# Low parts of the U and V tiles in the dense stage: from GpSimd to the vector engine

## The chip, the cores and the metric

One core of one Trainium2 chip runs the whole program. Its engines are TensorE (PE, matmuls), the vector engine (DVE), ScalarE (ACT), GpSimd (POOL) and SyncE (SP, which here only issues DMAs). The metric is the device time of one execution, in microseconds. Three runs of the kernel before took 3260.62, 3271.71 and 3278.69 us (median 3271.71).

## The reference

The reference is one layer of a hybrid backbone: two gated mixers, an output projection, and then a feed-forward block called PEER. Only the last part matters here:

```
def retrieve(xb):                                   # 128 tokens at a time, 1024 in all
    q = (xb @ wq).reshape(128, 8, 2, 128)
    s = einsum('tphq,phkq->tphk', q, keys)          # 2 x 128 keys per head
    top_s, top_i = top_k(s, 16)
    ...                                             # 16 best pairs per head: idx, softmax g
    act = gelu(einsum('tpkd,td->tpk', u_tab[idx], xb))
    return einsum('tpk,tpkd->td', g * act, v_tab[idx])
```

Each token has 8 heads with 16 experts each, 128 in all, out of a table of 16384 experts. An expert is a row of U (1024 numbers) and a row of V (1024 numbers). The result goes through a gate, a residual addition and a final RMSNorm.

## The kernel before

The eight blocks of 128 tokens are split. Three blocks (the gather blocks, A) fetch the rows of their experts from memory. Five blocks (the dense blocks, B, 640 tokens) multiply with the whole U and V tables on TensorE, with a weight of zero for every expert that a token did not choose.

*The gather* is a generator (`gather_all`) of 3 x 128 steps, one per block and expert position. A step fetches, for each of the 128 tokens, one row of U and V (128 x 2048 numbers) by an indirect DMA that GpSimd issues (L936), two steps ahead, into one of four buffers `uv`. The vector engine multiplies the U half with the hidden state and sums (L983); ScalarE makes the activation from the sum (L948, L949); one step later the vector engine adds activation times V half to the accumulator `acc` (L961). The fetch into a buffer waits for the addition L961 that read it last. The gather's steps are spread over the other work by a count of time (`ticks`).

*The dense side* goes through the experts in 128 chunks of 128. `u_side(c)` multiplies one U chunk with the hidden state of the five blocks (48 matmuls, L1017); ScalarE's gelu of that is `w` (L1058). 84 of the chunks are done before the dense stage and wait in memory; the other 44 are done in it. `weights(c)` multiplies `w` with the routing weights (vector engine, L1376). The V product adds `w` times the V chunk to the output (L1403).

*High and low parts.* Each matmul operand of full precision is split in two: ScalarE rounds the tile to the matmul's type (`uh`, `vh`, `wh`), and a subtraction gives the rest, the low part (`ul`, `vl`, `wl`). A product is three matmuls: high x high, high x low, low x high. In the kernel before, GpSimd makes `ul` (L1043) and `vl` (L1369, and L1362 for the last five tiles), the vector engine makes `wl` (L1380).

*The dense stage* begins at about 1889 us. It goes through 16 groups of eight chunks; each group has two halves (the two halves of V's 1024 columns). In a half-group TensorE does eight steps of 5 x 3 matmuls into five PSUM banks of six; at its end the vector engine adds the five banks to the output accumulator (L1410). The second half also makes the next group's weights and, for some chunks, their U product. In step n the kernel issues, behind the matmuls of the first token block, the rounding and the low part of the V tile for step n + 2 (`v_prep`, three buffers each for `vh` and `vl`), and SP loads the raw tile for step n + 7 (five buffers). In the last group there is no next group, and the vector engine and GpSimd finish the residual.

The order of the instructions on each engine is the order in which the program issues them: nothing is rearranged.

Of the kernel before, what the change touches and what calls it, by code (L numbers as in the profile page):

```python
# [7 lines left out]
F32 = mybir.dt.float32  # L8
# [6 lines left out]
ALU = mybir.AluOpType  # L15
# [845 lines left out]
def peer(tc, A, F, order, ng, out, ahi, alo, eh, ga, h2s, h2_load, early=84, rho=0.42, rhog=0.33, ratio=1.35, lead=6.0, sige=0.2):  # L861
# [5 lines left out]
    V, S, T, G, Y = nc.vector, nc.scalar, nc.tensor, nc.gpsimd, nc.sync  # L867
    banks, ident, dr, rstd_of = [F["bank"]], F["ident"], F["dr"], F["rstd_of"]
    bank = lambda name: banks[0](name)
# [51 lines left out]
    def settle(n):  # L921

        t = row("acc")
        for h in range(2):
            S.activation(t[:, h * 512:h * 512 + 512], accs[n][:, h * 512:h * 512 + 512], AF.Copy)
        accs[n] = t
# [92 lines left out]
            if kt % 2:  # L1019
                yield 2 * 3 * sum(b - a for a, b in cuts) / 2400.0  # L1020

    us, wr, ubank, ulim = {}, {}, [bank], [early + 1]

    first = [c for c in range(P) if (c + 1) * early // P != c * early // P]
    plan = first + [c for c in range(P) if c not in first]
# [9 lines left out]
    def u_prep(c):  # L1035
        if c >= P or isinstance(us[c], tuple):
            return
        uh = up.tile([P, KT, P], F32R, tag="uh", name="uh")
        ul = up.tile([P, KT, P], F32R, tag="ul", name="ul")
        for n, ur in enumerate(us[c]):  # L1040
            k = slice(4 * n, 4 * n + 4)
            S.activation(uh[:, k], ur, AF.Copy)  # L1042
            G.tensor_tensor(ul[:, k], ur, uh[:, k].bitcast(F32), op=ALU.subtract)  # L1043
        us[c] = (uh, ul)

    def u_side(c, ahead):

        cuts = cuts_of(nd)
        pts = [ubank[0]("ua") for _ in cuts]
        for n, d in enumerate(project(pts, None, us[c][0], us[c][1], bhi, blo, cuts)):  # L1050
            if ahead and n == 0:
                u_prep(c + 1)
            if ahead and n == 1:
                u_load(c + (3 if c + 1 < early else 2))
            yield d
        w = wr[plan[c]] = up.tile([P, nd], F32, tag="we", name="w", bufs=3)
        for pt, (a, b) in zip(pts, cuts):
            S.activation(w[:, a:b], pt[:, :b - a], AF.Gelu)  # L1058
# [133 lines left out]
    def prime():  # L1192

        u_load(0)
        u_load(1)
        u_load(2)
        u_prep(0)
# [116 lines left out]
    acc = hB2.tile([P, nb, D], F32, name="accB")  # L1314
    ru[0] = es.enter_context(tc.tile_pool(name="ru2", bufs=2))
    ulim[0] = P
    for n in list(accs):
        if accs[n] is psum[0]:
            settle(n)
# [6 lines left out]
    with tc.tile_pool(name="vhl", bufs=3) as vp, tc.tile_pool(name="whl", bufs=GRP) as wp, \  # L1326
            tc.tile_pool(name="gw", bufs=2) as gw:
        ws, vs, gts, vr = {}, {}, {}, {}
# [23 lines left out]
        def v_last(n):  # L1352

            if not halves:
                for _ in range(2):
                    th, tl = (up.tile([P, KT, P], F32R, tag=t, name="v" + t).rearrange("p (a k) e -> p a (k e)", a=2)
                              for t in ("uh", "ul"))
                    halves.extend((th[:, a], tl[:, a]) for a in range(2))
                halves.append([up.tile([P, nd], F32R, tag="we", name="vw", bufs=3)[:, :512] for _ in range(2)])
            vh, vl = vs[n] = halves.pop(0)  # L1360
            S.activation(vh, vr[n], AF.Copy)
            G.tensor_tensor(vl, vr.pop(n), vh.bitcast(F32), op=ALU.subtract)  # L1362

        def v_prep(n):
            if n < len(vseq) - NX:
                vh = vp.tile([P, 512], F32R, tag="vh", name="vh")
                vl = vp.tile([P, 512], F32R, tag="vl", name="vl")
                S.activation(vh, vr[n], AF.Copy)  # L1368
                G.tensor_tensor(vl, vr.pop(n), vh.bitcast(F32), op=ALU.subtract)  # L1369
                vs[n] = (vh, vl)  # L1370

        def weights(c):
# [39 lines left out]
        def v_ahead(n):  # L1412
            v_prep(n + 2)
            if n + 7 < len(vseq) - NX:
                v_load(n + 7)
# [40 lines left out]
        for c in groups[0]:  # L1456
            produce(c)
            if c == 2:
                for n in range(2):
                    v_prep(n)  # L1460
                    v_load(n + 5)
        n = 0
        for g, group in enumerate(groups):
            nxt = groups[g + 1] if g + 1 < len(groups) else []
            for h in range(2):
# [3 lines left out]
                for i, c in enumerate(group):  # L1469
                    for b in range(nb):  # L1470
                        v_mm(pos[b], n, c, b, i == 0, i == len(group) - 1)
                        if nxt and i == len(group) - 1 and b >= HOLD:
                            owed[0] += t1 * share_of * (1.0 if h else ratio)
                        elif nxt:
                            ticks(t1, share_of * (1.0 if h else ratio))
                        else:
                            k = i * nb + b
                            if k < cut:
                                rest(cut - k)
                            j = k - cut  # L1480
                            if j >= 0 and j % 3 == 0 and j // 3 < nb:
                                x1_load(j // 3)
                            j -= 8
                            if j >= 0 and j % 3 == 0 and j // 3 < nb:
                                residual(j // 3, 1)
                        if b == 0:
                            v_ahead(n)
                        if b == 1:
                            weigh()
                        if b == 3 and not nxt:  # L1490
                            if 1 <= i < 1 + NX:
                                v_last(len(vseq) - NX - 1 + i)
                            if i < NX:
                                v_load(len(vseq) - NX + i)
                    n += 1
                    if h and i < len(nxt):
                        produce(nxt[i])
                for b in range(nb):
                    v_add(g, h, b, pos[b])

        v_prep(n + 2)

        def second(b, po):
# [28 lines left out]
def whole(tc, A, out, ng=8, dbg=None):  # L1532
# [32 lines left out]
    e2.close()  # L1565
    es.close()
    peer(tc, A, r, order, ng, out, ahi, alo, eh, ga, h2s, h2_load)
    r["es"].close()

# [55 lines left out]
```

## Time and profile before

| | |
|---|---|
| runs, us | 3260.62, 3271.71, 3278.69 |
| profiled execution, us | 3258.37 |
| its span, us | 3256.6 |
| mean granted TensorE clock | 0.945 |
| busy share: PE, DVE, ACT, POOL | 89%, 79%, 40%, 49% |
| dense stage | about 1889 us to the end |

Busy shares are averages over stages that are limited by different things. The stage around the change is read from its own stretch, by who waits for whom. An engine's instruction can overlap the end of the one before it by some 0.08 us, so that the time from start to start is a little less than the duration.

### The profile page before, as it was taken

To read this page: it belongs to the slowest core of one execution; us is meant where nothing else is said; L and a number is where in the kernel's file an instruction comes from. 1 tells how busy PE (TensorE), PEld (TensorE's weight loads), DVE (VectorE), ACT (ScalarE), POOL (GpSimd) and SP (SyncE) were. 2 spreads that over 40 slices of the span, in tenths; PEclk is the share of its full clock that TensorE was granted. 3 is DMA by queue.
4 is the path that set the end of the run, shared out by engine and by line. 5 is a ranking of instruction groups with operands and counts; after the bars stand their busy time and mean duration, and the time that the engine had idled before them with its cause. 6 is when DMAs were issued, how large, how long until landed. Compare 5 with 4: busy or idle time off the path is not lost.

```text
span 3256.6 us, 47765 instructions
## 1 busy us (share of the span) xinstructions
PE 2895.9 (89%) x17321; PEld 2560.1 (79%) x17321; DVE 2583.2 (79%) x4467; ACT 1304.8 (40%) x2909; POOL 1581.0 (49%) x1102
## 2 busy tenths in 40 slices
PE   6999989998988987798888889989998899999897
PEld 3899887777988987688887877777777777778775
DVE  6633418666898999999999778888888788888886
ACT  4622224453444455455555433333333233333232
POOL 1000002333456766644343466666665566667664
PEclk9999999799998998899999999999999899999999
DMA  5254437345377876689898999999988898999883
GB/s 204 71 182 143 142 110 261 123 134 178 120 261 267 286 261 238 218 283 322 314 320 310 353 318 318 315 319 310 311 301 308 302 321 305 321 315 320 305 294 126
DMA packets 374381, 831.44 MB, mean 255 GB/s; under 512 B 27001, under 2 KB 198649, under 8 KB 324737
## 3 DMA queue, kind: packets, MB, share of 16 engines
q0 software_dynamic: 57600, 411.07, 35.0%
q1 hardware_dynamic: 292624, 347.74, 33.6%
q10 hardware_dynamic: 23920, 69.59, 5.5%
q8 instruction: 136, 2.23, 0.3%
q14 instruction: 101, 0.82, 0.1%
HBM read 729.38 MB, written 98.91 MB: 254 GB/s over the span
## 4 chain that ended last, share of the span: by engine, by line
DVE 21%; issue 11%; PE 10%; POOL 9%; DMA 5%; ACT 1%; SPq 0%; POOLq 0%; DVEq 0%; ACTq 0%
PE po L1403 7%; POOL vl L1369 4%; DVE ol L1296 4%; POOL uv L936 4%; DVE uv L983 4%; PE ua L1017 3%; DVE acc L961 3%; DMA uv<-uv,idx 3%; DVE accP L961 2%; DVE oh L1297 2%; DVE oh L1295 2%; DVE o L1294 2%; DVE w L1376 1%; DMA vr<-uv 1%; ACT wh L1379 1%
## 5 line engine op out<-in xcount | busy, mean ns | idle before, releaser
L936 POOL DMA_INDIRECT uv<-uv,idx x384 | 512.9, 1336 | 548.2 <-DVE accP L961 237.3
L983 DVE SCALAR_TENSOR_TENSOR uv<-uv,h2a 128x1024 f32<-128x1024 f32 x351 | 543.9, 1550 | 106.7 <-DMA uv<-uv,idx 106.5
L1403 PE MATMUL po<-vh,wh 128*128 128x512 f32 x1255 | 509.5, 406 | 118.4 <-DVE accB L1410 106.0
L1403 PE MATMUL po<-vl,wh 128*128 128x512 f32 x1255 | 507.1, 404 | 16.4 <-POOL vl L1369 16.4
L1017 PE MATMUL ua<-hBhi,uh 128*128 128x320 f32 x2048 | 487.2, 320 | 36.9 <-ACT uh L1042 30.3
L1403 PE MATMUL po<-vh,wl 128*128 128x512 f32 x1255 | 503.8, 401 | 0.0
L1017 PE MATMUL ua<-hBhi,ul 128*128 128x320 f32 x2048 | 478.4, 315 | 21.2 <-POOL ul L1043 20.9
L1369 POOL TENSOR_TENSOR vl<-vr,vh 128x512 fp32r<-128x512 f32 x251 | 387.2, 1545 | 198.4 <-ACT vh L1368 177.9
L1017 PE MATMUL ua<-hBlo,uh 128*128 128x320 f32 x2048 | 477.1, 315 | 0.0
L1043 POOL TENSOR_TENSOR ul<-ur,uh 128x512 fp32r<-128x512 f32 x256 | 391.9, 1553 | 171.3 <-ACT uh L1042 164.4
L961 DVE SCALAR_TENSOR_TENSOR acc<-uv,act,acc 128x1024 f32<-128x1024 f32 x237 | 398.3, 1681 | 8.5 <-ACT act L949 8.5
L1403 PEld LDWEIGHTS po<-vh,wh 128*128 128x128 f32 x1255 | 246.2, 196 | 179.8 <-DVE accB L1410 115.4
L1017 PEld LDWEIGHTS ua<-hBhi,uh 128*128 128x128 f32 x2048 | 352.0, 194 | 44.3 <-ACT uh L1042 32.9
L1017 PEld LDWEIGHTS ua<-hBhi,ul 128*128 128x128 f32 x2048 | 351.3, 193 | 26.9 <-POOL ul L1043 26.9
L1017 PEld LDWEIGHTS ua<-hBlo,uh 128*128 128x128 f32 x2048 | 352.6, 193 | 0.0
L1403 PEld LDWEIGHTS po<-vl,wh 128*128 128x128 f32 x1255 | 246.3, 196 | 72.0 <-POOL vl L1369 22.3
L1403 PEld LDWEIGHTS po<-vh,wl 128*128 128x128 f32 x1255 | 245.5, 196 | 53.0
L1379 ACT ACTIVATE wh<-w 128x640 fp32r<-128x640 f32 x128 | 94.6, 739 | 465.5 <-DVE w L1376 465.5
L1368 ACT ACTIVATE vh<-vr 128x512 fp32r<-128x512 f32 x251 | 156.5, 625 | 186.7 <-PE po L1403 156.1
L948 ACT ACTIVATE act<-act 128x1 f32<-128x1 f32 x384 | 76.1, 198 | 353.8 <-DVE uv L983 352.1
L468 POOL MEMSET v<- 128x4 f32 x20 | 2.0, 105 | 419.1 <-PE tm L207 383.7
L1380 DVE TENSOR_TENSOR wl<-w,wh 128x640 fp32r<-128x640 f32 x128 | 113.3, 885 | 104.8 <-ACT wh L1379 100.8
(375 smaller groups left out, 5920.5 us busy)
## 6 DMA issues: line engine op xcount, KB each, us to landing
ur<-uC SPq DMA_DIRECT2D x256, 256.0 KB
vr<-uv SPq DMA_DIRECT2D x256, 256.0 KB
d_G<-gtl ACTq DMA_DIRECT2D x80, 512.0 KB
gch<-d_G SPq DMA_DIRECT2D x64, 640.0 KB
d_A<-w ACTq DMA_DIRECT2D x84, 320.0 KB
w<-d_A SPq DMA_DIRECT2D x84, 320.0 KB
wm<-w_mod SPq DMA_DIRECT2D x32, 512.0 KB
qraw<-wq SPq DMA_DIRECT2D x32, 512.0 KB
```

Source lines behind the costliest of these rows:

```text
L936: G.indirect_dma_start(out=t.rearrange("p a d -> p (a d)"), out_offset=None, in_=A["uv"], in_offset=bass.IndirectOffsetOnAxis(ap=idxs[n][: ...
L948: S.activation(acts[i], acts[i], AF.Gelu)
L961: V.scalar_tensor_tensor(acc, v, act, acc, op0=ALU.mult, op1=ALU.add)
L983: V.scalar_tensor_tensor(t, t, 1.0, h2s[n], op0=ALU.mult, op1=ALU.mult, accum_out=acts[i])
L1017: T.matmul(pt[:, :b - a], l[:, kt], m[:, kt, a:b], start=(kt == 0 and wi == 0), stop=(kt == KT - 1 and wi == 2))
L1043: G.tensor_tensor(ul[:, k], ur, uh[:, k].bitcast(F32), op=ALU.subtract)
L1296: V.tensor_tensor(ol, oh, pairs(glT, b, t0), op=ALU.mult)
L1368: S.activation(vh, vr[n], AF.Copy)
L1369: G.tensor_tensor(vl, vr.pop(n), vh.bitcast(F32), op=ALU.subtract)
L1379: S.activation(wh, w, AF.Copy)
L1380: V.tensor_tensor(wl, w, wh.bitcast(F32), op=ALU.subtract)
L1403: T.matmul(po, st[:, b * P:(b + 1) * P], m, start=(start and wi == 0), stop=(stop and wi == 2))
```

## The change

In the dense stage the subtractions that make `ul` and `vl` move from GpSimd to the vector engine. Before the dense stage `ul` stays on GpSimd. Nothing else is altered; the subtractions stand at the same places of the program.

```
-    us, wr, ubank, ulim = {}, {}, [bank], [early + 1]
+    us, wr, ubank, ulim, usplit = {}, {}, [bank], [early + 1], [G]
...
             S.activation(uh[:, k], ur, AF.Copy)
-            G.tensor_tensor(ul[:, k], ur, uh[:, k].bitcast(F32), op=ALU.subtract)
+            usplit[0].tensor_tensor(ul[:, k], ur, uh[:, k].bitcast(F32), op=ALU.subtract)
...
     ulim[0] = P
+
+    usplit[0] = V
...
             S.activation(vh, vr[n], AF.Copy)
-            G.tensor_tensor(vl, vr.pop(n), vh.bitcast(F32), op=ALU.subtract)
+            V.tensor_tensor(vl, vr.pop(n), vh.bitcast(F32), op=ALU.subtract)
...
                 S.activation(vh, vr[n], AF.Copy)
-                G.tensor_tensor(vl, vr.pop(n), vh.bitcast(F32), op=ALU.subtract)
+                V.tensor_tensor(vl, vr.pop(n), vh.bitcast(F32), op=ALU.subtract)
```

The vector engine's queue in the first half of a group, from the five additions on, in the kernel before (`uv`, `act`, `acc` are the gather, `w` and `wl` a weight):

```order
L1410 TENSOR_TENSOR accB<-accB,po 128x512 x5
L983 SCALAR_TENSOR_TENSOR uv,act<-uv,h2a 128x1024
L961 SCALAR_TENSOR_TENSOR acc<-uv,act,acc 128x1024
L1376 TENSOR_TENSOR w<-w,gch 128x640
L1380 TENSOR_TENSOR wl<-w,wh 128x640
L983 SCALAR_TENSOR_TENSOR uv,act<-uv,h2a 128x1024
L961 SCALAR_TENSOR_TENSOR acc<-uv,act,acc 128x1024
L983 SCALAR_TENSOR_TENSOR uv,act<-uv,h2a 128x1024
L961 SCALAR_TENSOR_TENSOR acc<-uv,act,acc 128x1024
```

The same place now (line numbers behind the change are two higher, so L1412 is the former L1410, L1371 the former L1369):

```order
L1412 TENSOR_TENSOR accB<-accB,po 128x512 x5
L983 SCALAR_TENSOR_TENSOR uv,act<-uv,h2a 128x1024
L961 SCALAR_TENSOR_TENSOR acc<-uv,act,acc 128x1024
L1371 TENSOR_TENSOR vl<-vr,vh 128x512
L1378 TENSOR_TENSOR w<-w,gch 128x640
L1382 TENSOR_TENSOR wl<-w,wh 128x640
L983 SCALAR_TENSOR_TENSOR uv,act<-uv,h2a 128x1024
L961 SCALAR_TENSOR_TENSOR acc<-uv,act,acc 128x1024
L1371 TENSOR_TENSOR vl<-vr,vh 128x512
L983 SCALAR_TENSOR_TENSOR uv,act<-uv,h2a 128x1024
L961 SCALAR_TENSOR_TENSOR acc<-uv,act,acc 128x1024
L1371 TENSOR_TENSOR vl<-vr,vh 128x512 x2
```

One subtraction of a V tile stands in each of the eight steps between the gather's instructions. GpSimd's queue at about the same place, before (`uv` is a fetch):

```order
L936 DMA uv<-uv,idx_7051 128x2048
L1369 TENSOR_TENSOR vl<-vr,vh 128x512
L936 DMA uv<-uv,idx_7051 128x2048
L1369 TENSOR_TENSOR vl<-vr,vh 128x512
L1043 TENSOR_TENSOR ul<-ur,uh 128x512 x2
L936 DMA uv<-uv,idx_7051 128x2048 x2
L1369 TENSOR_TENSOR vl<-vr,vh 128x512 x2
```

And now, from the last U tile before the dense stage to the residual at the end:

```order
L1043 TENSOR_TENSOR ul<-ur,uh 128x512 x2
L936 DMA uv<-uv,idx_7051 128x2048 x108
L936 DMA uv<-uv,idx_7052 128x2048 x128
L1445 TENSOR_TENSOR accB<-accB,ft 128x512
L1446 TENSOR_TENSOR accB<-accB,fx 128x512
```

All fetches of the dense stage now stand directly behind one another.

## Rows read from the trace of the kernel before

**Rows 1.** Busy us (and instructions) of PE, PEld, DVE, ACT, POOL by stretch; PEclk, DMA share, GB/s

```profile
1840.00:1880.00 40.00, 37.42 (x253) 36.76 (x252) 18.07 (x20) 12.96 (x35) 22.34 (x17) 1.00 1.01 380
1896.00:3216.00 1320.00, 1186.48 (x5692) 1015.10 (x5690) 1110.39 (x1117) 420.91 (x1033) 867.62 (x567) 0.95 0.89 307
```

**Rows 2.** Waits of PE, 1896 to 3216: us in total, times, longest us

```profile
PE po L1403 <- DVE accB L1410: 106.0, 21, 7.8
```

**Rows 3.** Waits of DVE, same stretch

```profile
DVE wl L1380 <- ACT wh L1379: 97.6, 119, 2.0
DVE uv L983 <- DMA uv<-uv,idx: 86.0, 53, 4.1
```

**Rows 4.** DVE by line, same stretch: busy us, mean ns | idle before, releaser

```profile
L961 DVE SCALAR_TENSOR_TENSOR acc<-uv,act,acc 128x1024 f32<-128x1024 f32 x234 | 394.4, 1685 | 1.7 <-ACT act L949 1.7
L983 DVE SCALAR_TENSOR_TENSOR uv<-uv,h2a 128x1024 f32<-128x1024 f32 x234 | 387.5, 1656 | 86.1 <-DMA uv<-uv,idx 86.0
L1376 DVE TENSOR_TENSOR w<-w,gch 128x640 f32<-128x640 f32 x124 | 152.3, 1228 | 6.7 <-ACT w L1058 6.7
L1380 DVE TENSOR_TENSOR wl<-w,wh 128x640 fp32r<-128x640 f32 x124 | 109.8, 886 | 101.6 <-ACT wh L1379 97.6 <-issue 4.0
L1410 DVE TENSOR_TENSOR accB<-accB,po 128x512 f32<-128x512 f32 x140 | 85.9, 677 | 0.0
```

**Rows 5.** Chain that ended last, a piece: start us, us, what

```profile
2197.07 6.83 PE po L1403 x30
2203.90 7.04 PE ua L1017 x48
```

**Rows 6.** DVE in order of time, one half-group: start us, us, instruction, [idle before]

```profile
2239.73 3.07 DVE L1410 TENSOR_TENSOR accB<-accB,po 128x512 f32<-128x512 f32 x5
2242.72 1.22 DVE L983 SCALAR_TENSOR_TENSOR uv<-uv,h2a 128x1024 f32<-128x1024 f32 x1
...
2243.86 1.28 DVE L961 SCALAR_TENSOR_TENSOR acc<-uv,act,acc 128x1024 f32<-128x1024 f32 x1
2245.06 0.82 DVE L1376 TENSOR_TENSOR w<-w,gch 128x640 f32<-128x640 f32 x1
...
2247.43 1.22 DVE L983 SCALAR_TENSOR_TENSOR uv<-uv,h2a 128x1024 f32<-128x1024 f32 x1
...
2251.94 1.27 DVE L961 SCALAR_TENSOR_TENSOR acc<-uv,act,acc 128x1024 f32<-128x1024 f32 x1
2253.14 2.31 DVE L983 SCALAR_TENSOR_TENSOR uv<-uv,h2a 128x1024 f32<-128x1024 f32 x1
...
2265.31 1.58 DVE L983 SCALAR_TENSOR_TENSOR uv<-uv,h2a 128x1024 f32<-128x1024 f32 x1 [4.10 <-DMA uv<-uv,idx]
...
2272.86 0.67 DVE L1410 TENSOR_TENSOR accB<-accB,po 128x512 f32<-128x512 f32 x1
```

**Rows 7.** Gather lines, 1896 to 3216: ns min/median/max, first and last start, forms

```profile
L983 DVE SCALAR_TENSOR_TENSOR uv<-uv,h2a x234: 1208/1225/3228, 1898.3 to 3172.6; 128x1024 f32<-128x1024 f32 x117
L961 DVE SCALAR_TENSOR_TENSOR acc<-uv,act,acc x234: 1271/1282/2382, 1900.5 to 3178.3; 128x1024 f32<-128x1024 f32 x117
```

**Rows 8.** POOL in order of time, same half-group

```profile
2251.14 1.69 POOL L936 DMA_INDIRECT uv<-uv,idx  x1 [1.35 <-DVE acc L961]
2252.85 3.75 POOL L1369 TENSOR_TENSOR vl<-vr,vh 128x512 fp32r<-128x512 f32 x2
2256.74 1.76 POOL L936 DMA_INDIRECT uv<-uv,idx  x1
```

**Rows 9.** POOL by line, 1896 to 3216

```profile
L1369 POOL TENSOR_TENSOR vl<-vr,vh 128x512 fp32r<-128x512 f32 x248 | 382.2, 1543 | 198.4 <-ACT vh L1368 177.9 <-ACT act L948 14.8 <-DMA fx<-d_x 2.0
L1043 POOL TENSOR_TENSOR ul<-ur,uh 128x512 fp32r<-128x512 f32 x82 | 147.1, 1814 | 78.7 <-ACT uh L1042 78.6
```

**Rows 10.** Multiplication of two SBUF tiles in the tail, whole run

```profile
L1443 DVE TENSOR_TENSOR accB<-accB,ft x5: 679/1757/1772, 3198.1 to 3216.9; 128x512 f32<-128x512 f32 x5
```

**Rows 11.** Waits of ACT, 1896 to 3216

```profile
ACT vh L1368 <- PE po L1403: 156.1, 85, 2.9
```

## The prediction

> **What bounds the kernel now.** The views were read in this order: the page's busy shares, the busy time of each engine in stretches, the waits by engine, the groups by line for the vector engine and GpSimd, and the timeline of one half-group. The change acts from about 1889 us on, so only the dense stage counts. In its 1320 us from 1896 to 3216 TensorE is busy 1186 us, the vector engine 1110 us and GpSimd 868 us, and the DMA engines are at 0.89 of their time [rows 1]. No engine is full, so the reader has to look at who waits for whom.
>
> TensorE's longest wait is 106 us, for the additions that empty its PSUM banks (L1410, vector engine) [rows 2]. The vector engine waits 97.6 us for ScalarE's rounding of a weight (L1380) and 86.0 us for gathered rows [rows 3]. What it does not wait for says most: its 140 additions L1410 have 0.0 us of idle time before them [rows 4]. Whenever it comes to them, TensorE has long finished. The vector engine, with its busy time and its short waits, is therefore the late engine at nearly every half-group's end, and TensorE stands until it arrives. A half-group is eight weight chunks times five token blocks. Each chunk gives a block three matmuls, so a half is 120 of them; 30 take 6.83 us, so it needs 27.3 us, and a U chunk 7.04 us more [rows 5]. The half from 2239.73 to 2272.86 has no U chunk and took 33.1 us [rows 6].
>
> Much of the vector engine's busy time is not work. Its two gather instructions have medians of 1225 and 1282 ns [rows 7] but means of 1656 and 1685 ns [rows 4]. The timeline shows why. A product that starts at 2253.14 takes 2.31 us; GpSimd has just begun a pair of low parts, at 2252.85, which runs 3.75 us. An addition at 2251.94 takes 1.27 us although GpSimd issues a fetch from 2251.14 on, for 1.69 us [rows 6, 8]. So GpSimd's subtractions hold the vector engine up, and its fetches do not.
>
> **The change part by part.** *Leaves GpSimd:* 248 V and 82 U low parts in this stretch [rows 9] (five more of the last V tiles lie in the tail). *Arrives on the vector engine:* the same 330 subtractions, 128x512, each behind ScalarE's rounding. The trace has no such subtraction of two SBUF tiles there. The nearest row is the multiplication of two SBUF tiles of that size, 679 ns at best [rows 10]; L1410 of that size takes 677 ns alone [rows 4], and five in a row take 3.07 us [rows 6], so one more in a row costs (3.07 - 0.677) / 4 = 0.60 us, as ends overlap the next start. The two ends are 330 x 0.60 = 198 us and 330 x 0.679 = 224 us. I take 198, since the queue runs without gaps most of the time.
>
> *What goes with them:* the blocking. By the unblocked prices (the medians; 0.82 us for a 128x640 multiplication, from 2245.06 [rows 6], taken for L1380 too) and the means of [rows 4] that is 234 x (1.656 - 1.225) = 101, 234 x (1.685 - 1.282) = 94, 124 x (1.228 - 0.82) = 51 and 124 x (0.886 - 0.82) = 8, in all 254 us. Net on the vector engine: 198 - 254 = -56 us, with -30 as the other end.
>
> The page Perfetto Trace Analysis of the Trainium skill, section Optimizing Scalar/DVE Operations, advises the reverse: when the vector engine is saturated, hand work to ScalarE or even GpSimd; it adds that the two share an SBUF read port, so that it might not help. Taken alone, the first half would make this change a loss of the whole 198 us; the 2.31 us beside 1.27 us in the trace speaks for the second half. The sum above uses neither.
>
> *Fetches:* GpSimd's queue now holds fetches alone until the tail. Before, a fetch stands behind subtractions: that of 2256.74 behind the pair of 2252.85 [rows 8]. The product at 2265.31 then waits 4.10 us for its rows [rows 6]; the buffer that the fetch needed had been free since the addition of 2251.94 ended, at 2253.2, so the delay was some 3.5 us, nearly all of that wait. The 53 waits average 86.0 / 53 = 1.6 us. The gain lies between 0 and 86: less than all, because a stage some 80 us shorter must move the same bytes at 307 x 1320 / 1240 = 327 GB/s, and the DMA engines were at 0.89. They did reach 380 GB/s at share 1.01 for 40 us with another mix [rows 1]. I take half, -43 us.
>
> *New wait:* a V low part now waits, in the vector engine's own queue, for ScalarE's rounding two chunks ahead, and that for TensorE to give a buffer back (three of them). ScalarE waited 156.1 us, 85 times, for that [rows 11]. Behind the subtraction now stand the next products and additions of the gather, the weights, and the additions L1410, for which TensorE waits, and fetches wait for the gather's additions. Where the vector engine is the late one, the rounded tile lies ready and the wait is nothing; the 0.0 us before L1410 says that it is late at each half's end. Where it is early, TensorE sets the pace and the wait is mostly free. The ends are 0 and 156 us; nearer the first, I take +20. U low parts follow their roundings while the gather or a weight's subtraction runs, at no cost. If the cover is gone, they share this price. SP's loads of raw tiles wait for the subtraction on another engine than before; they are issued five chunks ahead, so I add nothing.
>
> *Sum:* -56 - 43 + 20 = -79 us. The profiled execution took 3258.4 us, so 3179; the median of the runs shown, 3271.7, lies 13.3 us above it, so 3193 on the scale of the runs.
>
> A check by one half: that from 2239.73 has seven gather steps, spaced 1.14 us (2242.72 to 2243.86) plus 1.20 us (2243.86 to 2245.06), one weight of 2.37 us with the rounding that it waits for (2245.06 to 2247.43), and five additions of 0.60: 16.4 + 2.4 + 3.0 = 21.8 us. Eight low parts bring it to 26.6 us, below TensorE's 27.3 and well below the 33.1 of now [rows 6]. So such a half would become TensorE's. Halves with three U chunks (48.4 us on TensorE) come out about level.
>
> **The rivals.** *1. TensorE becomes the bound.* All gather waits go and the new wait costs nothing: -56 - 86 = -142 us, 3130. For it: 27.3 against 26.6 us in that half. Against: that is more than the 106 us that TensorE loses at L1410 [rows 2], and a slack of two chunks does not cover every burst.
>
> *2. The DMA engines take the gain.* Rows land later as the demand rises, and the vector engine waits at the gather as long as it has saved: waits of 86 + 56 us or so, about 3272, no change. For it: share 0.89. Against: the 380 GB/s, and fetches that start earlier.
>
> *3. Slower: the queue locks.* The vector engine inherits ScalarE's 156 us, and cannot use that time for the gather: -56 + 156 = +100 us, 3372. It decides from the point where more than 56 us (99, if the fetches gain their 43) of those waits fall in stretches where the vector engine later proves the late one. For it: products that could run stand behind a subtraction whose input is not there. Against: 0.0 us before L1410.
>
> *4. The blocking does not come from the subtractions* but from something that stays, as the fetch's own writes: no relief, +198 us, 3470. Against it stands the addition of 2251.94. (The advice of the Trainium skill's page Perfetto Trace Analysis, to unload a saturated vector engine, would lead here; the trace so far sides with its second half.)
>
> **How the numbers follow.** The forecast's own range goes from -56 - 86 + 20 = -122 to -56 + 0 + 20 = -36 us, which is 3150 to 3236, at 0.60; rival 1 (below 3150) 0.08; between forecast and no change 0.03; rival 2 0.13; rival 3 0.13; rival 4 0.03. Half a per cent, 16 us, is about what a measurement of this kernel can tell from no change. Faster is 0.60 + 0.08 + 0.03 = 0.71; within, 0.13; slower, 0.16. The range for 8 in 10 takes part of rival 1 and rival 2: 3140 to 3285.
>
> **What would show it.** Right: L983 and L961 near 1.23 and 1.28 us on average; the low parts near 0.68 us each; fewer than 50 us of gather waits; TensorE's waits for L1410 well below 106 us; a higher granted clock than 0.95. Wrong: long waits of the low parts for ScalarE (rival 3), gather waits above 86 us with the DMA share near 1 (rival 2), or means that stay near 1.66 us (rival 4).

## The result and the profile after

The changed kernel takes 3171.64 us (median of four runs, 3167.59 to 3174.0), the kernel before 3268.47 (four runs; the forecast had started from the median of three of them, 3271.71). The ratio is 0.9701, interval 0.967 to 0.9732: 97 us less. The profiled execution of the changed kernel took 3167.59 us (span 3165.8) against 3258.4 before, 91 us less. The forecast was 3193.

The dense stage ends some 90 us earlier, so its window is 1896 to 3126 here. First the busy time of the engines in two stretches (columns as in [rows 1]):

```profile
1840.00:1880.00 40.00, 37.41 (x252) 36.73 (x252) 18.64 (x22) 12.91 (x35) 18.56 (x16) 1.00 1.02 383
1896.00:3126.00 1230.00, 1169.20 (x5732) 1004.61 (x5731) 1055.46 (x1464) 424.48 (x1035) 277.68 (x234) 0.98 0.92 329
```

The vector engine executes 347 instructions more than before in such a window, and yet is busy 55 us less: 1055 us, where it was 1110. GpSimd's busy time falls from 868 to 278 us. The transfers reach 329 GB/s, the rate that the prediction asked of them (327), at a share of 0.92. The stretch ahead of the dense stage reads as before.

The vector engine by line, same window, answers to [rows 4]:

```profile
L961 DVE SCALAR_TENSOR_TENSOR acc<-uv,act,acc 128x1024 f32<-128x1024 f32 x234 | 299.3, 1279 | 0.2 <-ACT act L949 0.2
L983 DVE SCALAR_TENSOR_TENSOR uv<-uv,h2a 128x1024 f32<-128x1024 f32 x234 | 285.0, 1218 | 32.4 <-DMA uv<-uv,idx 32.1
L1371 DVE TENSOR_TENSOR vl<-vr,vh 128x512 fp32r<-128x512 f32 x249 | 169.3, 684 | 25.3 <-ACT vh L1370 24.8
L1382 DVE TENSOR_TENSOR wl<-w,wh 128x640 fp32r<-128x640 f32 x126 | 104.0, 825 | 103.4 <-ACT wh L1381 103.4
L1378 DVE TENSOR_TENSOR w<-w,gch 128x640 f32<-128x640 f32 x126 | 102.9, 817 | 3.4 <-DMA gch<-d_G 3.4
L1412 DVE TENSOR_TENSOR accB<-accB,po 128x512 f32<-128x512 f32 x145 | 89.0, 679 | 0.0
L1043 DVE TENSOR_TENSOR ul<-ur,uh 128x512 fp32r<-128x512 f32 x82 | 52.7, 684 | 0.0
```

Every line with two operands in SBUF has fallen to its unblocked price: the products from a mean of 1656 ns to 1218, the gather's additions from 1685 to 1279, the weights' multiplication from 1228 to 817. L1412, which has one operand in PSUM, stands at 679 ns, as its 677 before. That no single blocked instruction is left shows in the smallest, median and largest duration, against maxima of 3228 and 2382 ns in [rows 7]:

```profile
L983 DVE SCALAR_TENSOR_TENSOR uv<-uv,h2a x234: 1208/1218/1227, 1904.4 to 3076.6; 128x1024 f32<-128x1024 f32 x117
L961 DVE SCALAR_TENSOR_TENSOR acc<-uv,act,acc x234: 1273/1279/1285, 1905.5 to 3083.2; 128x1024 f32<-128x1024 f32 x117
```

The waits of TensorE and of ScalarE (us in total, times, longest) answer to [rows 2] and [rows 11]:

```profile
PE po L1405 <- DVE accB L1412: 45.4, 17, 5.7
```

```profile
ACT vh L1370 <- PE po L1405: 160.9, 83, 3.2
```

TensorE stands 45 us for the additions where it stood 106. ScalarE waits for a free buffer as long as before, but the vector engine has taken over only 24.8 us of that. GpSimd by line:

```profile
L936 POOL DMA_INDIRECT uv<-uv,idx x232 | 276.4, 1192 | 908.2 <-DVE acc L961 880.8 <-DVE acc L959 12.0 <-DVE uv L983 9.8
```

Its fetches now wait for one thing, the buffer that the addition L961 gives back.

The half-group that [rows 6] showed from 2239.73 to 2272.86 (33.1 us) is this one now, the vector engine in order of time:

```profile
2216.03 3.07 DVE L1412 TENSOR_TENSOR accB<-accB,po 128x512 f32<-128x512 f32 x5
...
2221.36 0.68 DVE L1371 TENSOR_TENSOR vl<-vr,vh 128x512 fp32r<-128x512 f32 x1
2221.96 0.81 DVE L1378 TENSOR_TENSOR w<-w,gch 128x640 f32<-128x640 f32 x1
2223.58 0.82 DVE L1382 TENSOR_TENSOR wl<-w,wh 128x640 fp32r<-128x640 f32 x1 [0.81 <-ACT wh L1381]
...
2238.89 1.23 DVE L983 SCALAR_TENSOR_TENSOR uv<-uv,h2a 128x1024 f32<-128x1024 f32 x1 [2.11 <-DMA uv<-uv,idx]
...
2245.00 3.07 DVE L1412 TENSOR_TENSOR accB<-accB,po 128x512 f32<-128x512 f32 x5
```

It takes 29.0 us. The low part costs 0.60 us from start to start (2221.36 to 2221.96), as worked out. Over 28 half-groups, from the first additions to the last, the sum fell from 1199.9 to 1111.0 us.

### The profile page after: what moved, and what is told of

The parts are those of the page before. It is cut to its first block, busy times and chain, and to the rows that moved or that the text cites. A ratio compares the mean times of both kernels' runs of the same rounds, so it can differ in the third digit from the quotient of the medians.

```text
span 3165.8 us, 47649 instructions
## 1 busy us (share of the span) xinstructions
PE 2882.2 (91%) x17321; PEld 2555.5 (81%) x17321; DVE 2518.5 (80%) x4809; ACT 1307.1 (41%) x2909; POOL 973.6 (31%) x760
## 4 chain that ended last, share of the span: by engine, by line
issue 27%; DVE 17%; POOL 8%; PE 4%; DMA 1%; ACT 0%; POOLq 0%; SPq 0%; DVEq 0%
POOL uv L936 8%; DVE ol L1296 4%; PE po L1405 3%; DVE uv L983 3%; DVE accP L961 2%; DVE oh L1297 2%; DVE oh L1295 2%; DVE o L1294 2%; PE ua L1017 2%; DMA vr<-uv 1%; DMA uv<-uv,idx 1%; DVE acc L961 0%; DVE vl L1371 0%; DVE accB L1412 0%; DMA ft<-d_mod 0%
## 5 line engine op out<-in xcount | busy, mean ns | idle before, releaser
L936 POOL DMA_INDIRECT uv<-uv,idx x384 | 454.5, 1184 | 1299.1 <-DVE acc L961 891.5
L1405 PE MATMUL po<-vh,wh 128*128 128x512 f32 x1255 | 498.8, 397 | 49.7 <-DVE accB L1412 45.4
L1017 PE MATMUL ua<-hBhi,uh 128*128 128x320 f32 x2048 | 492.1, 322 | 39.0 <-ACT uh L1042 26.6
L1405 PE MATMUL po<-vl,wh 128*128 128x512 f32 x1255 | 498.4, 397 | 12.1 <-DVE vl L1371 12.0
L1405 PE MATMUL po<-vh,wl 128*128 128x512 f32 x1255 | 495.3, 395 | 0.0
L983 DVE SCALAR_TENSOR_TENSOR uv<-uv,h2a 128x1024 f32<-128x1024 f32 x351 | 437.4, 1246 | 49.3 <-DMA uv<-uv,idx 48.9
L961 DVE SCALAR_TENSOR_TENSOR acc<-uv,act,acc 128x1024 f32<-128x1024 f32 x237 | 303.2, 1279 | 0.2 <-ACT act L949 0.2
L1043 POOL TENSOR_TENSOR ul<-ur,uh 128x512 fp32r<-128x512 f32 x170 | 236.6, 1415 | 79.8 <-ACT uh L1042 75.5
L1381 ACT ACTIVATE wh<-w 128x640 fp32r<-128x640 f32 x128 | 94.6, 739 | 396.8 <-DVE w L1378 395.2
L1370 ACT ACTIVATE vh<-vr 128x512 fp32r<-128x512 f32 x251 | 156.6, 625 | 161.3 <-PE po L1405 160.9
L961 DVE SCALAR_TENSOR_TENSOR accP<-uv,act,accP 128x1024 f32<-128x1024 f32 x144 | 184.6, 1282 | 15.1 <-ACT act L949 15.1
L1371 DVE TENSOR_TENSOR vl<-vr,vh 128x512 fp32r<-128x512 f32 x251 | 170.9, 685 | 25.3 <-ACT vh L1370 24.8
L1278 ACT ACTIVATE gtl<-gb 128x512 f32<-128x512 f32 x160 | 160.3, 1111 | 71.6 <-PE gb L1276 62.8
```

The lines of the kernel that those rows point to most:

```text
L936: G.indirect_dma_start(out=t.rearrange("p a d -> p (a d)"), out_offset=None, in_=A["uv"], in_offset=bass.IndirectOffsetOnAxis(ap=idxs[n][: ...
L961: V.scalar_tensor_tensor(acc, v, act, acc, op0=ALU.mult, op1=ALU.add)
L983: V.scalar_tensor_tensor(t, t, 1.0, h2s[n], op0=ALU.mult, op1=ALU.mult, accum_out=acts[i])
L1017: T.matmul(pt[:, :b - a], l[:, kt], m[:, kt, a:b], start=(kt == 0 and wi == 0), stop=(kt == KT - 1 and wi == 2))
L1043: usplit[0].tensor_tensor(ul[:, k], ur, uh[:, k].bitcast(F32), op=ALU.subtract)
L1278: S.activation(gt[:, :, tt:tt + 4].rearrange("p e t -> p t e"), pt.rearrange("p (t e) -> p t e", e=P), AF.Copy, scale=1.0 / 4096.0)
```

## The experiments

Times are medians; "before" beside a run is the kernel before on the same chip. The edits are against the changed kernel and are shown shortened. The kernel before took 3265 to 3269 us beside all of these runs, so they are also compared with the changed kernel's 3171.64 directly.

**Only the V parts, only the U parts.** Two halves of the change, to see whether each does its share.

```
-    usplit[0] = V                                  (V parts only: U stays on GpSimd)
```

> Only the V low parts move to the vector engine; GpSimd keeps the 82 U low parts of the dense stage. Theory (GpSimd's subtractions block the vector engine, each for more than the 0.60 us that it costs there): three quarters of the change, so some 3195 us (3180 to 3215), with L983 and L961 still between 1.25 and 1.40 us on average, since a quarter of the subtractions stays. Rival (the fetches that no longer queue behind subtractions are most of the gain): gather waits fall to about 40 us and the time is within 10 us of the full change.

```
-            V.tensor_tensor(vl, vr.pop(n), ...)    (U parts only: V back on GpSimd,
+            G.tensor_tensor(vl, vr.pop(n), ...)     at both places)
```

> Only the U low parts of the dense stage move; GpSimd keeps the 249 V low parts. Theory: a quarter of the change, some 3245 us (3230 to 3260), with means of L983 and L961 near 1.5 to 1.6 us. Rival (the gain is not proportional to the subtractions moved, it needs an empty GpSimd): no change, 3260 to 3280.

Measured: V alone 3204.68 us, ratio 0.9812 (0.9787 to 0.9837), 63 us less than before; U alone 3240.91, ratio 0.9928 (0.9908 to 0.9947), 27 us less. They add to 90 of the 97. The gather's lines with V alone, and then with U alone:

```profile
L961 DVE SCALAR_TENSOR_TENSOR acc<-uv,act,acc 128x1024 f32<-128x1024 f32 x235 | 340.6, 1450 | 3.9 <-ACT act L949 3.9
L983 DVE SCALAR_TENSOR_TENSOR uv<-uv,h2a 128x1024 f32<-128x1024 f32 x235 | 323.0, 1375 | 34.8 <-DMA uv<-uv,idx 34.3
```

```profile
L961 DVE SCALAR_TENSOR_TENSOR acc<-uv,act,acc 128x1024 f32<-128x1024 f32 x235 | 369.6, 1573 | 1.1 <-ACT act L949 0.9
L983 DVE SCALAR_TENSOR_TENSOR uv<-uv,h2a 128x1024 f32<-128x1024 f32 x235 | 351.6, 1496 | 79.8 <-DMA uv<-uv,idx 79.6
```

The products' means fall by steps with the number of subtractions on GpSimd: 1656 ns with all 330, 1496 with the 248 of V, 1375 with the 82 of U, 1218 with none. The steps are not in proportion: with V alone the additions' 1450 ns lie above the 1.25 to 1.40 us expected. The waits for rows behave otherwise: 34 us once V's are gone, 80 while they stay.

**The subtractions back on GpSimd, beside the vector engine's.** This brings the blocking and the held queue back and keeps the new cost. GpSimd makes each low part once more, into the raw tile, which nobody reads afterwards.

```
             V.tensor_tensor(vl, vr[n], vh.bitcast(F32), op=ALU.subtract)
+            G.tensor_tensor(vr[n], vr[n], vh.bitcast(F32), op=ALU.subtract)   (for U alike)
```

> The changed kernel, and GpSimd subtracts once more behind each of the vector engine's 331 subtractions, into the dead raw tile; the output is the same. Theory (blocking): the means of L983 and L961 return to about 1.65 us, the vector engine gets some 250 us more, and the time is 3380 us (3320 to 3440), above the kernel before. Rival (the gain came from moving work between queues, not from the port): GpSimd had the time free, so 3172 to 3220.

Measured: 3386.32 us, ratio 1.0378 (1.0351 to 1.0404), 215 us more than the changed kernel and 6 above the 3380 expected. The gather's lines from 1896 us to the end:

```profile
L961 DVE SCALAR_TENSOR_TENSOR acc<-uv,act,acc 128x1024 f32<-128x1024 f32 x235 | 399.9, 1702 | 0.0
L983 DVE SCALAR_TENSOR_TENSOR uv<-uv,h2a 128x1024 f32<-128x1024 f32 x235 | 360.7, 1535 | 59.0 <-DMA uv<-uv,idx 58.9
```

Against the changed kernel these two lines alone are longer by 235 x (0.423 + 0.317) = 174 us, and the waits for rows by 27 us. So the blocking is most of the 215 us here. The run still takes the blocking and the queue together, and GpSimd's subtractions now wait for the vector engine's (437 us) and not, as in the kernel before, for ScalarE's roundings; the next runs part these.

**Only the queue.** GpSimd's work behind each of the vector engine's subtractions is three memsets of the dead raw tile, 0.53 us each.

```
             V.tensor_tensor(vl, vr[n], vh.bitcast(F32), op=ALU.subtract)
+            for _ in range(3):
+                G.memset(vr[n], 0.0)                                          (for U alike)
```

> The changed kernel, and GpSimd does three memsets of the dead raw tile behind each of the 331 subtractions, so that fetches stand behind work again, but work that reads nothing; the output is the same. Theory: L983 and L961 stay near 1.22 and 1.28 us; only the gather waits rise, from 32 to between 50 and 90 us, and the time to 3190 us (3172 to 3230). Rival (any work of GpSimd blocks the vector engine): as with the second subtraction, above 3300 us.

Measured: 3252.63 us (ten runs), ratio 0.9955 (0.9935 to 0.9976). This missed: 81 us above the changed kernel, where 18 had been expected. The blocking is gone as expected (products 1222 ns, additions 1280), but the vector engine waits 117.4 us for rows:

```profile
L983 DVE SCALAR_TENSOR_TENSOR uv<-uv,h2a 128x1024 f32<-128x1024 f32 x236 | 288.3, 1222 | 118.0 <-DMA uv<-uv,idx 117.4
```

A doubt stood against it: these memsets wait for the vector engine's subtraction (335 us of waits on GpSimd for V's tiles up to 3216 us), which the subtractions of the kernel before did not; they waited for ScalarE's rounding. So the queue was held in another way. The next run took that away.

```
+    def again(raw, hi):             (called where GpSimd's subtraction stood; scrap is 128 x 112)
+        G.tensor_tensor(scrap[:, 0:1], raw[:, 0:1], hi[:, 0:1].bitcast(F32), op=ALU.subtract)
+        for _ in range(9):          (five in the run after this one)
+            G.memset(scrap, 0.0)
```

> The changed kernel, and where GpSimd's subtraction stood it now does work of about the same length that reads no second SBUF tile at length: one subtraction of a single column (so that it waits for ScalarE's rounding, as before, and not for the vector engine) and nine memsets of 112 columns into a small scrap tile, about 1.5 us in all. Theory A (a fetch that stands behind GpSimd's own work comes late, whatever that work is; the run with memsets behind the vector engine's subtraction showed +81): the vector engine's waits for fetched rows come to 60 to 100 us instead of 32.1, and the time to about 3215. Theory B (those +81 came because GpSimd's work there waited for the vector engine, later than it ever did in the kernel before): waits for rows near 35 us, time 3172 within 10. Both: the products stay at 1.22 and 1.28 us.

Measured: 3323.59 us, ratio 1.0168 (1.0142 to 1.0194). Neither theory had that: 152 us above the changed kernel. The waits for rows are the longest of all runs, with the products unblocked:

```profile
L983 DVE SCALAR_TENSOR_TENSOR uv<-uv,h2a 128x1024 f32<-128x1024 f32 x235 | 287.5, 1224 | 191.5 <-DMA uv<-uv,idx 191.4
```

GpSimd in order of time in this run shows why:

```profile
2507.98 0.96 POOL L936 DMA_INDIRECT uv<-uv,idx  x1 [0.53 <-issue]
2508.97 0.68 POOL L1039 TENSOR_TENSOR scrap<-vr,vh 128x1 f32<-128x1 f32 x1
2509.71 2.19 POOL L1041 MEMSET scrap<- 128x112 f32 x9
```

One place holds the queue for 2.9 us, not the 1.5 us that was aimed at. An estimate from these rows: 333 such places and some 230 fetches of 1.18 us come to about 1240 of the 1404 us from 1896 to 3300, so GpSimd has little time left. The dose was wrong, so it was halved.

> The run with GpSimd's one-column subtraction and memsets again, with five memsets in place of nine: those nine took 2.2 us with the column's 0.2 to 0.5 us ahead of them, 2.6 us at each of 333 places, where the kernel before had a subtraction of 1.54 to 1.81 us; five come to about 1.2 + 0.4 = 1.65 us, its length. Theory (the fetches' wait grows with the time that the queue is held): at 1.65 us between the changed kernel (0 us, 3171) and the run with nine (2.6 us, 3323): waits for fetched rows 60 to 110 us, time about 3225 (3200 to 3260). Rival (no cost until the queue is over-full): below 3185, waits for rows under 50 us.

Measured: 3232.45 us, ratio 0.989 (0.9847 to 0.9933), 61 us above the changed kernel.

```profile
L961 DVE SCALAR_TENSOR_TENSOR acc<-uv,act,acc 128x1024 f32<-128x1024 f32 x234 | 299.4, 1280 | 1.1 <-ACT act L949 1.1
L983 DVE SCALAR_TENSOR_TENSOR uv<-uv,h2a 128x1024 f32<-128x1024 f32 x234 | 285.4, 1220 | 94.8 <-DMA uv<-uv,idx 94.6
```

Here the waits for rows, 94.6 us, are near the 86.0 of [rows 3], at unblocked prices. A place holds 0.47 + 5 x 0.243 = 1.7 us of work, about the 1.54 and 1.81 us of the subtractions in [rows 9]. Against the changed kernel the waits rise by 62.5 us with five memsets, by 85.3 with the three of the raw tile and by 159.3 with nine; the time rises by 61, 81 and 152. In these runs a microsecond of waiting for rows was nearly a microsecond of time, and a queue held for about as long as before cost about 60 us without any blocking.

**The cost twice.** Each low part made twice in a row by the vector engine, into the same tile.

```
             V.tensor_tensor(vl, vr[n], vh.bitcast(F32), op=ALU.subtract)
+            V.tensor_tensor(vl, vr[n], vh.bitcast(F32), op=ALU.subtract)      (for U alike)
```

> The changed kernel with each of the vector engine's 331 low parts made twice in a row into the same tile: the cost of the change doubled without any further relief. Theory (the vector engine is the late one, and a low part in a row costs it 0.60 us): +199 us less the 32 us in which it waits for fetched rows and some of its other waits, about 3172 + 160 = 3335 (3310 to 3375). Rival (TensorE has become the bound and the vector engine has room): below 3260.

Measured: 3356.13 us, ratio 1.0269 (1.0244 to 1.0295): 184 us more. The vector engine is still the late one. The waits for rows shrink to 2.7 us and those for ScalarE's rounding of V to 6.4, as they must if it comes later to everything. That the time is 21 us over the 3335 expected fits the pair:

```profile
2506.74 0.69 DVE L1373 TENSOR_TENSOR vl<-vr,vh 128x512 fp32r<-128x512 f32 x1
2507.46 0.69 DVE L1374 TENSOR_TENSOR vl<-vr,vh 128x512 fp32r<-128x512 f32 x1
2508.07 0.82 DVE L1381 TENSOR_TENSOR w<-w,gch 128x640 f32<-128x640 f32 x1
```

The second of a pair, which writes the tile that the first has just written, starts 0.72 us after it and not 0.60. So a pair adds 0.72 + 0.61 - 0.60 = 0.73 us, 331 of them 242 us, less 29 and 18 us of waits gone: 195, where 184 were measured.

**A gap filled.** The vector engine waits 0.81 us for ScalarE in each weight (the timeline above, 2223.58). The V low part of that step is put into this gap.

```
             S.activation(wh, w, AF.Copy)
+            while low:
+                low.pop()()            (the V low part due in this step, held back until here
                                        with the load of a raw tile that follows it)
             V.tensor_tensor(wl, w, wh.bitcast(F32), op=ALU.subtract)
```

> The changed kernel with the V low part, where a chunk's weights are due, put between the weight multiplication and the subtraction of wl on the vector engine's queue: there it waits 0.81 us for ScalarE's rounding of w, 103.4 us in all (126 times). If the vector engine is the late one, up to 0.6 us of each of about 120 gaps is filled, 70 us less what TensorE then holds (TensorE waits 45 us for the additions in all): about 3140 (3110 to 3160). Rival (the engines trade places: TensorE or the fetches take the gain): 3165 or more.

Measured: 3136.13 us, ratio 0.959 (0.9561 to 0.9619), 35 us less than the changed kernel and near the 3140 expected. From 1896 us to the end, in the profiled execution (3157.43 us, the longest of the four):

```profile
L1385 DVE TENSOR_TENSOR wl<-w,wh 128x640 fp32r<-128x640 f32 x128 | 105.7, 826 | 30.1 <-ACT wh L1382 30.1
L1379 DVE TENSOR_TENSOR w<-w,gch 128x640 f32<-128x640 f32 x128 | 105.2, 822 | 43.1 <-ACT w L1058 22.1 <-DMA gch<-d_G 20.2 <-issue 0.7
```

The waits of wl fell from 103.4 us to 30.1. New waits for `w` (22.1 us) and for the routing weights (20.2 us) give a part back.

**The U parts before the dense stage too.**

```
-    ..., usplit = ..., [early + 1], [G]
+    ..., usplit = ..., [early + 1], [V]
```

> The changed kernel with the U low parts on the vector engine from the start: 167 more, of the part before the dense stage. Cost 167 x 0.60 = 100 us there, where the vector engine is busy 947 of 1010 us; relief by the same rule (mean less median of its operations of two SBUF tiles there) 105 to 120 us. Theory (each subtraction on GpSimd blocks the vector engine for about as long as it would take it itself): 3172 within 25. Rival (no blocking there, the cost remains): about 3270.

Measured: 3135.8 us, ratio 0.958 (0.9546 to 0.9615), 36 us less than the changed kernel: better than the break-even expected, and outside its 25. Two lines of the vector engine from 880 to 1840 us, in the changed kernel and then in this run:

```profile
L1296 DVE TENSOR_TENSOR ol<-oh,glT 128x1024 f16<-128x1024 f16 x80 | 128.0, 1601 | 2.8
L839 DVE TENSOR_TENSOR oh<-oh 128x1024 bf16<-128x1024 bf16 (+2 forms) x48 | 58.2, 1212 | 1.7
```

```profile
L1043 DVE TENSOR_TENSOR ul<-ur,uh 128x512 fp32r<-128x512 f32 x168 | 111.6, 706 | 15.8 <-ACT uh L1042 15.8
L1296 DVE TENSOR_TENSOR ol<-oh,glT 128x1024 f16<-128x1024 f16 x80 | 55.4, 692 | 2.8
L839 DVE TENSOR_TENSOR oh<-oh 128x1024 bf16<-128x1024 bf16 (+2 forms) x48 | 22.5, 470 | 1.6
```

L1296 gives back 73 us and L839 36 (this line had been left out of the estimate), together about what the 168 subtractions cost there, 112 us. All told the vector engine is busy 904 us of that stretch, where it was 927, with 279 instructions more in it, so some later work has moved in. The profiled executions (3143.86 and 3167.59 us) differ by 24 us only; the 36 are from the medians.

**Both.** The last two together:

> The changed kernel with both: the V low part in the gap ahead of wl (alone 35 us less) and the U low parts of the part before on the vector engine too (alone 35 us less). The two lie in different stretches of the program. If they add: 3100 (3085 to 3120). Rival (TensorE or the transfers, by then at 334 GB/s and a share of 0.94 in the dense stage, hold the end): 3120 or more.

Measured: 3108.86 us, ratio 0.95 (0.9456 to 0.9543). It is the fastest of all, 160 us below the kernel before and 63 below the changed one; of the 35 and 36, 71 together, 63 are left.

## Why the prediction was right

*The bound.* The vector engine was the late one, as read from the 0.0 us before its additions [rows 4], and it still is: 0.0 us before L1412 afterwards, and making each low part twice costs 184 us.

*The cost of the subtractions.* 198 us had been taken, 0.60 us for each. They last 684 ns and stand 0.60 us apart.

*The blocking.* Forecast -254 us. By the means after: 234 x (1.656 - 1.218) + 234 x (1.685 - 1.279) + 124 x (1.228 - 0.817) + 124 x (0.886 - 0.825) = 102 + 95 + 51 + 8 = 256 us. Rival 4 fell with it. That GpSimd's subtractions do it, and not that it is busy, the memsets show: GpSimd busy 756 us of 1230 with five at a place, the products at 1220 ns. The page SBUF — State Buffer of the Trainium skill, section Who interferes with whom, states this: a vector instruction with two inputs in SBUF collides with a GpSimd instruction that reads SBUF, not with one that only writes. The runs agree (1656 ns beside subtractions, 1220 beside memsets), and so does L1410 with its one SBUF input, 677 ns before and 679 after. The one-column subtractions, which do read, lengthened nothing that the means show. No run was made for the number of inputs, but the kernel before has the comparison in it. From 880 to 1840 us, beside GpSimd's U subtractions among others, the same addition L961 has its accumulator in PSUM (`accP`), and so one SBUF tile to read; the product L983 has two:

```profile
L983 DVE SCALAR_TENSOR_TENSOR uv<-uv,h2a x110: 1203/1218/3110, 908.2 to 1836.6; 128x1024 f32<-128x1024 f32 x110
L961 DVE SCALAR_TENSOR_TENSOR accP<-uv,act,accP x139: 1260/1284/1334, 918.3 to 1835.4; 128x1024 f32<-128x1024 f32 x139
```

The longest of 139 such additions takes 1334 ns; with the accumulator in SBUF the longest is 2382 [rows 7].

*The fetches.* Forecast -43 us, half of what was possible. The waits fell from 86.0 to 32.1 us, by 54, and the queue held for about its old length by itself cost 61 us. This term was too small, by 11 us by the rows and by 18 by that run. The argument for taking half, that the transfers would not keep up, weighed too much: they rose to 329 GB/s. Nearly all of it belongs to V, as the two halves of the change show.

*The new wait.* +20 us was taken; 24.8 us stand in the rows, of ScalarE's 160.9. Rival 3 fell. The U low parts show no wait, as forecast, and TensorE waits 7.8 us for V's low parts, where it waited 15.0 us for GpSimd's. What the 24.8 us are worth was not tried by itself.

*Rivals 1 and 2.* TensorE did not become the bound, though the half-group looked so: 26.6 us against 27.3. Here the working was right but for one thing. The half took 29.0 us; without its 2.1 and 0.2 us of waits for rows that is 26.7. The forecast reckoned with waits for rows in its sum and left them out of its half. The DMA engines took none of the gain either.

*What is left.* By these rows, 199 - 256 - 54 + 25 is -86 us, where the forecast had -79; the profiled executions differ by 91. The rest stands in the last groups and at the ends. The 89 us of the 28 half-groups are 59 us of the vector engine's busy time and 30 us of its waits. Beside the terms above they hold the residual and the last two norms, which run on SBUF tiles too (about 10 us less), the waits for the residual's inputs (9.1 us before, none now), and the last five V low parts, with 8.2 us of new waits. The forecast had put those five into the tail; they lie ahead of it, inside the stretch of the rows. Before these half-groups the program is 7 us shorter, behind them 5 us longer.

The granted clock rose in the stage from 0.95 to 0.98, near the upper of its two levels (2.4 GHz), as TensorE stood less at the half-groups' ends; a matmul's busy time fell from 1186.48 / 5692 = 0.208 us to 1169.20 / 5732 = 0.204. What that is worth by itself was not tried.

Of the 21 us by which 3193 was too high, 12 are the sum's (79 us against 91), with the fetch term as its largest miss. The other 9 came with the scale and not with the mechanism: the forecast added the 13.3 us by which the profiled execution of before lay under its median, and that of the changed kernel lies only 4.1 us under its own.

## What to carry to other kernels

Compare mean and median of a line: when the mean stands far above, find in the timeline what runs beside the long ones, and price the move by what it stops (here 256 us) against what it costs at start-to-start spacing (199 us). Helping a busy engine with another that reads the same memory can cost it more than doing the work itself; the same move earlier in this program was worth another 36 us. A queue that issues fetches is best left free of other work, since each microsecond that the vector engine waited for rows here was nearly one of the total, and a wait of fixed length on the bound engine is a place to put work that has to be done anyway.

## What the runs showed of the hardware

Two subtractions of the vector engine that write the same tile one after the other stood 0.72 us apart, where those into different tiles stood 0.60 apart. On GpSimd, a memset of 128 x 112 had a busy time of 192 ns, but nine of them took 2.19 us, 243 ns each, and a subtraction of one column took 444 ns on average: short instructions there have a price that their size does not show (the nine also write one tile, one after the other, and times on GpSimd are rough). That is how the run with nine memsets came to hold the queue for twice the time intended.

```profile
L1041 POOL MEMSET scrap<- 128x112 f32 x3006 | 575.9, 192 | 172.9
L1039 POOL TENSOR_TENSOR scrap<-vr,vh 128x1 f32<-128x1 f32 x251 | 111.4, 444 | 56.4 <-issue 43.9 <-POOL scrap L1041 4.2 <-ACT act L948 1.3
```
